# Retention's state update: one 64x64 matmul per head in two column groups instead of one 128x128 per pair of heads

## The chip, the cores and the metric

The kernel runs on one core of one Trainium2 chip. The metric is the device time of one execution in microseconds, and the times of several executions are summarised by their median. TensorE (PE) does the matmuls and holds a weight tile that is loaded separately (PEld); VectorE (DVE), ScalarE (ACT) and GpSimd (POOL) work on SBUF and PSUM; SyncE (SP) issues most of the DMA transfers.

## The reference, cut to what matters

The program is a trunk of two layers over 1024 tokens of width 1024. Each layer has a normalisation, one input projection, three groups of heads (windowed attention, retention, gated linear attention), an output projection and a residual. Retention has four heads with key and value width 64 and works in chunks of 128 tokens:

```python
def step(state, inp):
    qi, ki, vi = inp
    sc = jnp.einsum('bhid,bhjd->bhij', qi, ki) * dmask
    intra = jnp.einsum('bhij,bhjv->bhiv', sc, vi)
    inter = jnp.einsum('bhid,bhdv->bhiv', qi * q_decay, state)
    new_state = chunk_decay * state + jnp.einsum('bhjd,bhjv->bhdv', ki * k_decay, vi)
    return new_state, intra + inter
```

The part that the change touches is the last sum: for each head a product of k (128 tokens by 64) and v (128 tokens by 64), contracted over the tokens, added to a state of 64 by 64. There are eight chunks in each layer; after the last one no state is needed, so there are seven updates in each of two layers, 14 in all.

## The kernel before

All 1024 tokens are cut into eight tiles of 128, which are also retention's chunks. A layer runs in this order: the gates (`gg`, `rg`), then retention's projections `rq`, `rk`, `rv` for pairs of tiles, then those of the linear attention and the attention, their cores, and the output projection. The weights come from DRAM in pieces of 256 KB into staging tiles `st`, of which there are five, and are split there into a high part (L145 on ACT or L147 on DVE, a cast) and a low part (L489 on DVE or POOL, a subtraction), both kept in `arena`.

The order of TensorE's instructions is the order in which the program records them. Side work (a chunk of retention, of attention, a normalisation) is written as generators that are put into a list of jobs; a planning clock `clk` is advanced by a cost for every recorded matmul (in `mult` at L161) and transpose (L176), and a job goes on when the clock has reached its due time, taken from a table of latencies `L`. So the side work is laid between the projections' matmuls by hand-set costs. The order on the other engines is made by a scheduler from the recorded program.

A chunk of retention is the job `ret_core(l, t, q, k, v)`. Its steps are: four transposes of q and k into one PSUM tile (L176); a copy to SBUF by ACT (key `rT`, L145); after a planned delay the scores, four matmuls of 64 contracted rows (L161, shown as `aux<-t 64*128`); the causal mask by DVE (L1055); then, once the previous state is there, for each pair of heads q times the state `stR` and the scores times v; and then the state update.

`stR` holds two pairs of heads, each as a 128 by 128 tile: the head's 64 by 64 state stands on the diagonal, and the other two blocks stay zero, so that one matmul of 128 contracted rows serves both heads of a pair. The update before multiplies the k of a pair (128 columns) by the v of the pair (128 columns) into 128 by 128 of PSUM (`pst`), whose off-diagonal blocks are not used. DVE adds the upper left and the lower right blocks to `stR` (L1074, twice) and multiplies all of it by the chunk's decay (L1076). k carries the inverse decay already (L1033). After the chunk, `head_norm_gate` normalises the output, and ACT and DVE write a high and a low half (L145, L845), which SP stores to `mixS`.

Two other places use groups of columns already: the linear attention's state update (`gla_core`, four heads with 32 columns each) and attention's product of probabilities and v (two groups of 64 columns). Before the matmuls of retention's scores, ACT's copy `rT` has to be done; ACT runs its instructions in its own order, among them casts of weights, the copy of v (key `rv`) and the high halves for `mixS`, whose buffers must have been stored before they are written again.

Of the kernel before, what the change touches and what calls it, by code (L numbers as in the profile page):

```python
# [14 lines left out]
ALU = mybir.AluOpType  # L15
AX = mybir.AxisListType

P = 128
# [71 lines left out]
def trunk(ctx: ExitStack, tc: tile.TileContext, ins, cst, out):  # L90
    nc = tc.nc
    V, A, G, T = nc.vector, nc.scalar, nc.gpsimd, nc.tensor
# [16 lines left out]
    def t2(dt=F32):  # L109
        return gp.tile([P, 512], dt, tag="t2", name=nm("t2"), bufs=B2)  # L110

    def t1(dt=F32):
        return gp.tile([P, 256], dt, tag="t1", name=nm("t1"), bufs=B1)
# [10 lines left out]
    def aux(dt=F32):  # L124
        return ps.tile([P, 512], dt, tag="aux", name=nm("aux"), bufs=8 - MMB)
# [17 lines left out]
    def copy(k, dst, src):  # L143
        if EN[k] == "A":
            A.activation(dst, src, AF.Copy)  # L145
        else:
            V.tensor_copy(dst, src)  # L147

    def dma(k, dst, src):
        {"S": nc.sync, "A": A, "P": G}[EN[k]].dma_start(dst, src)  # L150

    def h4(ap):
        return ap.rearrange("p (h q) -> p h q", h=4)
# [6 lines left out]
    def mult(dst, lhsT, rhs, start, stop, cost=None):  # L160
        T.matmul(dst, lhsT, rhs, start=start, stop=stop)  # L161
        if cost is not None:
            clk[0] += cost
            return
        n = 1
        for d in rhs.shape[1:]:
            n *= d
        c = n / 2400.0
        if rhs.dtype == F32R:
            c = max(c, 0.107 if lhsT.shape[-1] > 64 else 0.055)  # L170
        else:
            c = max(4 * c, 0.21 if n > 2 else 0.03)
        clk[0] += c

    def transp(dst, src, idn):
        T.transpose(dst, src, idn)  # L176
        clk[0] += 0.056 if src.dtype == F32R else 0.109

    def lat(key, l):

        return L[key + "@1"] if l and key + "@1" in L else L[key]
# [4 lines left out]
    def flag(name, lat=0.0):  # L186
        flags[name] = clk[0] + lat
# [661 lines left out]
    def head_norm_gate(l, t, po, gate, scale, eps, kt0):  # L849

        sq = t1()
        A.activation(sq, po, AF.Square)
        ss = small(4)
        V.tensor_reduce(ss, h4(sq), AX.X, ALU.add)
        r = rstd_of(ss, 4, scale, eps)
        g1 = t1()
        V.tensor_tensor(h4(g1), h4(po), r.unsqueeze(2).to_broadcast((P, 4, 64)), ALU.mult)  # L857
        eng("hng").tensor_tensor(g1, g1, gate, ALU.mult)  # L858
        yield lat("hn1", l)
        pt = aux()  # L860
        for j in range(2):
            transp(pt[:, j * P:(j + 1) * P], g1[:, j * P:(j + 1) * P], ident)
        store_mix(t, kt0, pt[:, 0:256].rearrange("p (k q) -> p k q", k=2), 2)
        flag(("mix", l, t, kt0), lat("hn2", l))
# [171 lines left out]
    def ret_core(l, t, q, k, v):  # L1036
        yield lat("rc1", l)
        pt = aux()
        for j in range(2):
            transp(pt[:, j * P:(j + 1) * P], q[:, j * P:(j + 1) * P], ident)  # L1040
            transp(pt[:, (2 + j) * P:(3 + j) * P], k[:, j * P:(j + 1) * P], ident)
        tt_ = t2()
        qT = tt_[:, 0:256]
        kTt = tt_[:, 256:512]
        copy("rT", tt_, pt)
        yield lat("rc2", l)
        sp = [aux(), aux()]
        for h in range(4):
            r = slice(64 * (h % 2), 64 * (h % 2) + 64)
            c = slice((h // 2) * P, (h // 2) * P + P)  # L1050
            mult(sp[h % 2][:, c], kTt[r, c], qT[r, c], True, True)
        sc = t2()
        scv = h4(sc)
        for c in range(2):
            V.tensor_tensor(scv[:, c:4:2], sp[c][:, 0:256].rearrange("p (h q) -> p h q", h=2),  # L1055
                            causal.unsqueeze(1).to_broadcast((P, 2, P)), ALU.mult)
        yield lat("rc3", l)
        if t > 0:
            yield (0.0, ("stR", l, t))
        po = aux()  # L1060
        for j in range(2):
            if t > 0:
                mult(po[:, j * P:(j + 1) * P], qT[:, j * P:(j + 1) * P], stR[:, j, :], True, False)
            for h in (2 * j, 2 * j + 1):
                mult(po[:, 64 * h:64 * h + 64], sc[:, h * P:(h + 1) * P], v[:, 64 * h:64 * h + 64],
                     t == 0, t == 0 or h % 2 == 1)
        if t < NT - 1:
            pst = aux()
            for j in range(2):
                mult(pst[:, j * P:(j + 1) * P], k[:, j * P:(j + 1) * P], v[:, j * P:(j + 1) * P], True, True)  # L1070
            for c in range(2):
                r = slice(64 * c, 64 * c + 64)
                blk = stR[r, :, 64 * c:64 * c + 64]
                V.tensor_tensor(blk, blk, pst[r, 0:256].rearrange("p (j n) -> p j n", j=2)[:, :, 64 * c:64 * c + 64],  # L1074
                                ALU.add)
            V.tensor_tensor(stR, stR, cdt.unsqueeze(2).to_broadcast((P, 2, P)), ALU.mult)  # L1076
            flag(("stR", l, t + 1), lat("rc4", l))
        sg = t1()
        dma("lsr", sg, srS[t])
        yield from head_norm_gate(l, t, po[:, 0:256], sg, 4.0 / 64.0, 4.0 * EPS, 4)  # L1080
# [59 lines left out]
    def layer(l):  # L1140
# [35 lines left out]
        for p in range(NP_):  # L1176
            last = p == NP_ - 1
            rr = {}
            for name in ("rq", "rk", "rv"):
                w = unit(l, name)  # L1180
                for tt in range(2):
                    t = 2 * p + tt
                    pm = mm()
                    project(pm[:, 0:256], l, t, w)
                    src = pm[:, 0:256]
                    if name == "rv":
                        v = t1()
                        copy("rv", v, src)
                        job(ret_core(l, t, rr[("rq", tt)], rr[("rk", tt)], v))
                    else:  # L1190
                        rr[(name, tt)] = ret_rot(t, src, qdec if name == "rq" else kdec)
                    pump()
                if last:
                    load(l, {"rq": "gqk", "rk": "gv", "rv": "kv"}[name])
# [169 lines left out]
```

## Time and profile before

| | |
|---|---|
| median of 3 runs | 1022.42 us (1018.75 to 1022.86) |
| the profiled execution's own time | 1017.62 us |
| its span, first to last instruction | 1015.6 us |
| granted TensorE clock, mean | 0.988 |
| TensorE busy | 984.0 us, 97% of the span |
| VectorE, ScalarE, GpSimd busy | 641.1, 387.8, 279.7 us |
| HBM read and written | 102.42 and 34.60 MB |

A row of the timeline gives the start, the length, the engine, the line of the program, the operation, what it writes and reads, the shape (rows*columns of the weights, then partitions x moving columns), the count, and, in brackets, the idle time before it with what ended it. Neighbouring instructions of one kind are merged into one row. A row of groups gives the count, the busy time, the mean length in ns, and the idle time before. A line can be that of a helper: every matmul has L161, and every copy made through one helper has L145 or L147. Matmuls overlap, so a length says less than the distance between two starts. A matmul on fp32 operands leaves two records.

### The profile page before, as it was taken

What the parts mean: (1) busy time and instruction counts of PE and PEld (TensorE: products, weight loads), DVE (VectorE), ACT (ScalarE), POOL (GpSimd) and SP (SyncE); (2) the same over time, 40 slices, a digit from 0 to 9 for tenths busy, and PEclk for the clock granted to TensorE, in tenths of its full rate; (3) what the DMA queues carried; (4) which work ended last, traced back from release to release, by engine and by line L of the source; (5) the groups of instructions that cost most, each with busy time, mean ns of one, the idle gap of its engine ahead of it and who ended that gap; (6) DMA issues with size and microseconds to landing.
All of it is one profiled execution on the core that took longest, in us unless ns stands there. A gap on an engine that the chain in (4) does not pass through costs nothing.

```text
span 1015.6 us, 19469 instructions
## 1 busy us (share of the span) xinstructions
PE 984.0 (97%) x7185; PEld 837.6 (82%) x7185; DVE 641.1 (63%) x1567; ACT 387.8 (38%) x1112; POOL 279.7 (28%) x310
## 2 busy tenths in 40 slices
PE   5899999999999999999999999999999999999997
PEld 1599999888998777778889999988899877777886
DVE  3778856858656778754676285685666576563322
ACT  2477311233322655633454332133322266653111
POOL 2342011434320335522243020132333134532000
PEclk8999999999999999999999999999999999999999
DMA  9842513624226355687455161342122323436753
GB/s 320 283 132 78 162 58 99 175 74 120 79 72 187 89 141 177 189 270 228 166 159 164 47 177 32 94 139 81 53 91 74 114 89 95 139 118 202 230 188 143
DMA packets 124555, 140.39 MB, mean 138 GB/s; under 512 B 12990, under 2 KB 95784, under 8 KB 124460
## 3 DMA queue, kind: packets, MB, share of 16 engines
q1 hardware_dynamic: 118764, 129.53, 41.8%
q10 hardware_dynamic: 5696, 9.62, 2.6%
q8 instruction: 56, 0.92, 0.4%
q14 instruction: 39, 0.32, 0.1%
HBM read 102.42 MB, written 34.60 MB: 135 GB/s over the span
## 4 chain that ended last, share of the span: by engine, by line
PE 85%; DVE 5%; DMA 2%; ACT 1%; issue 1%; POOL 1%; DVEq 0%; POOLq 0%; SPq 0%; ACTq 0%
PE mm L161 65%; PE aux L161 15%; PE aux L176 5%; DMA st<-in_w_mod_dram 2%; DVE arena L489 1%; DVE acc L361 1%; POOL sm L525 0%; ACT t L145 0%; DVE arena L147 0%; DVE mx L997 0%; POOL arena L489 0%; DVE t L858 0%; DMA st<-in_w_in_dram 0%; ACT L899 0%; DVE t L963 0%
## 5 line engine op out<-in xcount | busy, mean ns | idle before, releaser
L161 PE MATMUL mm<-arena,arena 128*128 128x256 f32 (+2 forms) x1824 | 302.5, 319 | 2.8 <-DVE t L871 2.0
L161 PE MATMUL mm<-arena 128*128 128x256 f32 (+2 forms) x1824 | 298.6, 318 | 2.8 <-ACT arena L594 1.8
L161 PEld LDWEIGHTS mm<-arena,arena 128*128 128x128 f32 x1824 | 254.8, 190 | 28.4 <-issue 4.4
L161 PEld LDWEIGHTS mm<-arena 128*128 128x128 f32 x1824 | 255.2, 191 | 25.5 <-ACT arena L594 2.0
L161 PE MATMUL mm<-arena,mx 128*128 128x512 f32 (+1 forms) x816 | 184.4, 384 | 0.0
L161 PEld LDWEIGHTS mm<-arena,mx 128*128 128x128 f32 x816 | 145.6, 188 | 33.7 <-issue 1.9
L525 POOL TENSOR_TENSOR sm<-sm,mhalf 128x1 f32<-128x1 f32 (+1 forms) x64 | 53.0, 828 | 316.3 <-DVE sm L524 309.7
L489 POOL TENSOR_TENSOR arena<-st,arena 128x512 fp32r<-128x512 f32 x58 | 81.9, 1420 | 110.2 <-ACT arena L145 88.4
L145 ACT ACTIVATE t<-aux 128x256 f32<-128x256 f32 (+2 forms) x112 | 52.2, 471 | 94.3 <-PE aux L176 76.4
L813 POOL TENSOR_TENSOR smx<-smx,sm 128x512 f32<-128x512 f32 x32 | 36.2, 1131 | 139.1 <-DVE sm L812 114.7
L809 ACT ACTIVATE smx<-smx,sm 128x129 f32<-128x129 f32 x128 | 50.0, 393 | 44.8 <-DVE sm L806 42.1
L145 ACT ACTIVATE arena<-st 128x512 fp32r<-128x512 f32 x82 | 48.8, 625 | 44.7 <-PE mm L161 20.2
L361 DVE SCALAR_TENSOR_TENSOR acc<-st,c_act,acc 128x512 f32<-128x512 f32 x60 | 49.1, 818 | 22.8 <-DMA st<-in_w_mod_dram 22.5
L176 PE MATMUL aux<-c_ident,t 128*128 128x128 f32 x288 | 48.2, 286 | 8.4 <-DVE t L556 5.9
L1124 DVE SCALAR_TENSOR_TENSOR t<-t,sm,t 128x512 f32<-128x512 f32 x32 | 26.9, 876 | 41.2 <-DMA t<-xs 20.5
L489 DVE TENSOR_TENSOR arena<-st,arena 128x512 fp32r<-128x512 f32 x54 | 51.0, 958 | 2.7 <-ACT arena L145 1.3
L1089 DVE TENSOR_TENSOR t<-mm,modg 128x512 f32<-128x512 f32 x30 | 20.7, 688 | 47.7 <-ACT t L1088 47.2
L176 PEld LDWEIGHTS aux<-c_ident,t 128*128 128x128 f32 x288 | 35.3, 146 | 14.7 <-DVE t L556 7.3
L1088 ACT ACTIVATE t<-mm 128x512 f32<-128x512 f32 x30 | 17.9, 595 | 73.7 <-DVE t L1124 37.4
L161 PEld LDWEIGHTS aux<-t,mx 32*128 32x128 f32 (+1 forms) x896 | 40.2, 187 | 5.3 <-issue 2.8
L161 PE MATMUL aux<-t,mx 32*128 32x32 f32 (+1 forms) x896 | 41.5, 272 | 1.1 <-DVE t L857 0.9
L588 ACT ACTIVATE t<-aux,mod,mod 128x128 f32<-128x128 f32 x68 | 26.0, 457 | 41.8 <-PE aux L176 18.7
(193 smaller groups left out, 1253.3 us busy)
## 6 DMA issues: line engine op xcount, KB each, us to landing
st<-in_w_in_dram SPq DMA_DIRECT2D x96, 256.0 KB
st<-in_w_mod_dram SPq DMA_DIRECT2D x64, 256.0 KB
mx<-mixS SPq DMA_DIRECT2D x32, 512.0 KB
mixS<-t SPq DMA_DIRECT2D x64, 128.0 KB
st<-in_w_out_dram SPq DMA_DIRECT2D x32, 256.0 KB
mixS<-t SPq DMA_DIRECT2D x32, 256.0 KB
wm<-in_w_mod_dram SPq DMA_DIRECT2D x12, 512.0 KB
t<-in_x_dram SPq DMA_DIRECT2D x24, 256.0 KB
```

The lines of the kernel that those rows point to most:

```text
L145: A.activation(dst, src, AF.Copy)
L161: T.matmul(dst, lhsT, rhs, start=start, stop=stop)
L176: T.transpose(dst, src, idn)
L361: V.scalar_tensor_tensor(acc, wt, c_act[:, k:k + 1], acc, ALU.mult, ALU.add)
L489: (G if first == 0 else eng(f"wlo{kc}")).tensor_tensor(wt[:, 1, 2 * kc:2 * kc + 2, 0:256], st, f(hi), ALU.subtract)
L525: G.tensor_tensor(r, r, mhalf[:, :w], ALU.pow)
L588: A.activation(hf[:, ks], at[kt], AF.Identity, scale=gain, bias=shift)
L809: A.activation(sm[:, h, :], sm[:, h, :], AF.Exp, bias=mx[:, h:h + 1], accum_out=sums[:, h:h + 1])
L813: eng("pn").tensor_tensor(sm[:, :, 0:128], sm[:, :, 0:128], rs.unsqueeze(2).to_broadcast((P, 4, P)), ALU.mult)
L1088: A.activation(yg, pm, AF.Square, accum_out=ss[:, nh:nh + 1])
L1089: V.tensor_tensor(yg, pm, modg[l][:, 512 * nh:512 * nh + 512], ALU.mult)
L1124: V.scalar_tensor_tensor(xt[j], yg[j], r, xt[j], ALU.mult, ALU.add)
```

## The change

The change replaces the two matmuls of a chunk's update by four. Each multiplies the 64 k columns of one head by the 64 v columns of the same head. The head with even number writes PSUM partitions 0 to 63, the one with odd number 64 to 127, so that the two heads of a pair stand in two groups of columns of the array; the pair's index picks the PSUM columns. DVE reads the same number of elements as before, now from 128 columns of PSUM. The planning cost is given as 0.1067 for each of the four, 0.427 for a chunk; before, two matmuls had 0.2133 each by the rule in `mult`, 0.427 as well.

```diff
             pst = aux()
             for j in range(2):
-                mult(pst[:, j * P:(j + 1) * P], k[:, j * P:(j + 1) * P], v[:, j * P:(j + 1) * P], True, True)
+                for c in range(2):
+                    h = slice(P * j + 64 * c, P * j + 64 * c + 64)
+                    mult(pst[64 * c:64 * c + 64, 64 * j:64 * j + 64], k[:, h], v[:, h], True, True, 0.1067)
             for c in range(2):
                 r = slice(64 * c, 64 * c + 64)
                 blk = stR[r, :, 64 * c:64 * c + 64]
-                V.tensor_tensor(blk, blk, pst[r, 0:256].rearrange("p (j n) -> p j n", j=2)[:, :, 64 * c:64 * c + 64],
-                                ALU.add)
+                V.tensor_tensor(blk, blk, pst[r, 0:P].rearrange("p (j n) -> p j n", j=2), ALU.add)
             V.tensor_tensor(stR, stR, cdt.unsqueeze(2).to_broadcast((P, 2, P)), ALU.mult)
```

## The prediction

> **What bounds the kernel now.** I read the page first: its span, the busy shares and the chain that ended last.
>
> ```profile
> span 1015.6 us, 19469 instructions
> PE 984.0 (97%) x7185; PEld 837.6 (82%) x7185; DVE 641.1 (63%) x1567; ACT 387.8 (38%) x1112; POOL 279.7 (28%) x310
> PEclk8999999999999999999999999999999999999999
> PE 85%; DVE 5%; DMA 2%; ACT 1%; issue 1%; POOL 1%; DVEq 0%; POOLq 0%; SPq 0%; ACTq 0%
> ```
>
> TensorE is busy for 97% of the span, has its full clock after the start and holds 85% of the chain. A change of its instruction stream is therefore worth what it does to TensorE's own time, plus what it does to the few waits of TensorE. The changed lines run in two stretches only, so the next views are the busy times there and TensorE's waits there.
>
> ```profile
> 120.00:206.00 86.00, 84.58 (x690) 79.63 (x688) 57.51 (x168) 21.44 (x44) 17.27 (x16) 1.00 0.37 111
> 606.00:692.00 86.00, 83.77 (x683) 78.72 (x683) 58.48 (x167) 19.82 (x41) 16.03 (x14) 1.00 0.35 102
> ...
> PE aux L161 <- ACT t L145: 0.6, 1, 0.6
> PE aux L176 <- DVE t L1033: 0.6, 1, 0.6
> ...
> PE aux L161 <- ACT t L145: 1.5, 2, 0.9
> PE aux L176 <- DVE t L1033: 0.6, 1, 0.6
> ```
>
> The first two rows give per stretch its length and the busy time (instructions) of PE, weight loads, DVE, ACT and POOL. TensorE works 84.6 of 86 us and 83.8 of 86. The four others name what its waits come from (total, times, longest; first stretch, then second): ACT's copy of the transposed q and k (L145), and DVE's k decay (L1033). Nothing in either list waits for `stR`, so the state update itself has slack, and DVE's three instructions on `stR` stay what they are.
>
> **The instructions replaced.** A 128x128 fp32 matmul is two records in the trace, so 28 matmuls are the 56 of the next row. After the change there are 56 matmuls, 112 records, with 64 weight columns and 64 moving columns. The durations overlap; what counts is the distance between weight loads.
>
> ```profile
> L161 PE MATMUL aux<-t,t 128*128 128x128 f32 x56 | 9.3, 288 | 0.0
> ...
> 128.89 0.97 PEld L161 LDWEIGHTS aux<-t,t 128*128 128x128 f32 x8
> 129.78 0.30 PEld L161 LDWEIGHTS mm<-arena,arena 128*128 128x128 f32 x2
> ```
>
> These eight loads are four for score times v (64 moving columns), then four for the state update (128 moving columns), and the next matmul's load starts 0.89 us after the first: 0.111 us each, with 64 columns streamed as with 128. So the load sets the pace. The old update costs 4 x 0.111 = 0.445 us a chunk. A load of 64 columns I take at half, 0.055, and of 32 at 0.028.
>
> The new shape is not in this trace, but its two neighbours are: the state update of the gated linear attention (four groups of 32 columns, 64 moving) and attention's product with v (two groups of 64 columns, 256 moving).
>
> ```profile
> 229.13 0.98 PEld L161 LDWEIGHTS aux<-t,mx 128*128 128x128 f32 x8
> 230.18 0.16 PEld L161 LDWEIGHTS aux<-t,t 128*32 128x32 f32 x8
> 230.43 0.19 PEld L161 LDWEIGHTS mm<-arena 128*128 128x128 f32 x1
> ...
> 348.12 0.20 PEld L161 LDWEIGHTS aux<-t,va 128*64 128x64 f32 x4
> 348.70 0.19 PEld L161 LDWEIGHTS mm<-arena,arena 128*128 128x128 f32 x1 [0.39 <-issue]
> ...
> L161 PEld LDWEIGHTS aux<-t,vd 128*64 128x64 f32 x112 | 8.0, 137 | 4.0
> ```
>
> - Groups run at once: four loads of some 137 ns each lie within 0.20 us.
> - Going in costs: the last of the eight full loads is at 229.13 + 7 x 0.111 = 229.91, and the first narrow load comes 0.27 later, 0.16 more than the pace. The array seems to empty before the shape changes.
> - The stay, from first narrow load to next full load, is 0.25 with two records a group of 64 columns streamed, and 0.58 with two of 256. With s for 64 columns streamed and d for the way out: 0.028 + 2s + d = 0.25 and 0.055 + 8s + d = 0.58, so s = 0.05 and d = 0.12.
>
> The new update has four records a group (two pairs of heads, two records each): 0.055 + 4 x 0.05 + 0.12 = 0.38 if the loads hide, 0.39 if they pace it. With the way in: 0.16 + 0.385 = 0.545 against 0.445, **+0.10 us a chunk**. Bounds: -0.22 (half the old time, no way in or out) and +0.33 (the groups one after the other: 0.055 x 8 + 0.05 + 0.12 + 0.16 - 0.445, rounded). I take 0.10, since both neighbours show the groups at once and the switch.
>
> In three of the 14 chunks the next work already has another shape (64-row groups), so the way out was paid before:
>
> ```profile
> 197.77 0.97 PEld L161 LDWEIGHTS aux<-t,t 128*128 128x128 f32 x8
> 198.87 0.52 PEld L161 LDWEIGHTS aux<-t 64*128 64x128 f32 x8
> ...
> 634.35 0.97 PEld L161 LDWEIGHTS aux<-t,t 128*128 128x128 f32 x8
> 635.45 0.52 PEld L161 LDWEIGHTS aux<-t 64*128 64x128 f32 x8
> ...
> 685.88 0.72 PE L161 MATMUL aux<-t 64*128 64x128 f32 x8 [0.95 <-ACT t L145]
> ```
>
> From the eighth load (197.77 + 0.78 = 198.55) to the next it is 0.32, 0.21 over the pace; the new update is then 0.11 cheaper, at 198 and at 635. The third, before 685.88, is hidden by a wait of 0.95 for ACT: 0. TensorE's own part: 11 x 0.10 - 2 x 0.11 = **+0.9 us**.
>
> **What moves beside it.** TensorE's order is unchanged. The lists of the two programs differ on the other engines in a few places at the last two chunks of each layer.
>
> ```profile
> 188.01 2.71 SPq L150 DMA_DIRECT2D mixS<-t  x2
> 190.83 3.27 SPq L150 DMA_DIRECT2D st<-in_w_in_dram  x4
> ...
> 673.96 2.74 SPq L150 DMA_DIRECT2D mixS<-t  x2
> 676.82 0.37 SPq L150 DMA_DIRECT2D st<-in_w_mod_dram  x1
> ...
> 678.59 0.87 ACT L145 ACTIVATE t<-aux 128x256 fp32r<-128x256 f32 x2 [1.27 <-DMA mixS<-t]
> ...
> 679.51 0.72 PE L161 MATMUL aux<-t 64*128 64x128 f32 x8 [0.55 <-ACT t L145]
> ...
> 184.88 0.37 SPq L150 DMA_DIRECT2D st<-in_w_in_dram  x1
> 187.69 0.63 ACT L145 ACTIVATE arena<-st 128x512 fp32r<-128x512 f32 x1 [2.13 <-DMA st<-in_w_in_dram]
> ```
>
> SP puts a 256 KB weight load ahead of the second 128 KB `mixS` store, at 188 to 191 and 674 to 677. ACT waits for that store (1.27 us) before it writes the buffer again, the copy of the transposed q and k is behind it in ACT's line, and TensorE waits for that copy (0.55). This is the chain on which the store's delay would reach TensorE. Bounds: 0, if the load is too late to matter, and 2.8 us, a whole load from issue (184.88) to use (187.69). The store took about 2 us from issue to use (issue over at 676.70, ACT free at 678.59), so 128 KB more is worth some 0.8 us and a 256 KB load ahead at most about twice that; it is issued earlier than the store, so part of it has passed. I take 0.4 at each place: **+0.8 us**.
>
> ```profile
> 684.44 0.63 ACT L145 ACTIVATE arena<-st 128x512 fp32r<-128x512 f32 x1 [0.72 <-PE aux L161]
> 684.98 0.36 ACT L145 ACTIVATE t<-mm 128x256 f32<-128x256 f32 x1
> 685.24 0.59 ACT L145 ACTIVATE t<-aux 128x512 f32<-128x512 f32 x1
> ...
> 180.68 0.41 DVE L147 CAST arena<-st 128x512 fp32r<-128x512 f32 x1
> 186.09 1.45 DVE L489 TENSOR_TENSOR arena<-st,arena 128x512 fp32r<-128x512 f32 x1
> ```
>
> On ACT the copy of v (684.98) moves ahead of the cast at 684.44, which takes 0.26 us (685.24 - 684.98) out of the way of the copy on which TensorE waits 0.95. But on SP the load of that cast moves behind a store. From -0.3 to +0.8: I take 0. On DVE a cast of weights (0.41) moves some twelve instructions later, at 180.68 and its twin at 667, and the subtraction behind it goes into a busier place, where one took 1.45. That is -0.4 to +1.0 before the k decay; TensorE would then wait longer there and shorter for ACT just after: 0. Swaps of DVE's `stR` lines with the norm's small ones are hidden by the slack of `stR`; gone, they cost an instruction's 0.4 each.
>
> **Sum.** +0.9 + 0.8 = +1.7 us. The profiled execution took 1017.62 us (span 1015.6), 4.8 under the median of the runs, so the same program would profile at 1019.3, and on the median 1022.42 it is **1024.1 us**. What this kernel's measurement can tell from no change is 0.5%, 5.1 us.
>
> **Rivals.**
> - Packing for free. The column groups halve the update and the switches hide: 14 x -0.22 = -3.1, 1019.3. For it: the groups do overlap. Against it: the 0.27 before the narrow loads, in a stream with no wait. The Trainium skill, TensorEngine Tiling (Array Packing), section Theoretical Speedup, gives up to 2x for a small dimension of 64, which is this case; its section Key Properties says that a switch of mode drains the array. By the first sentence alone the sum is 1019.3, and the row at 230.18 sides with the second.
> - The store behind the load, at full price. At both places ACT, and so TensorE, waits a whole load longer: 0.9 + 2 x 2.8 = 6.5, 1028.9, slower. It decides from 2.1 us on at each place (0.9 + 4.2 = 5.1), which needs a load that leaves just before the store. For it: ACT's wait ends with that store already. Against it: the load may go as soon as its buffer is free, well ahead.
> - The groups don't overlap, so that the change doesn't do what it says: 14 x 0.33 = 4.6, 1027.0. Against it: the four loads within 0.20 us.
>
> **How the numbers follow.** Forecast 0.62, all within 0.5%. Free packing 0.12 (0.08 within, 0.04 faster, if the runs fall 2 us lower as well). Store at full price 0.14, slower. No overlap 0.06 (0.04 within, 0.02 slower). Another 0.06, a third to each side, is for a median of runs that lie 4 us apart (1018.75 to 1022.86). Together: faster 0.06, within 0.76, slower 0.18. The range 1018.8 to 1028.0 takes in free packing and no overlap, and leaves out most of the store at full price.
>
> **What would show it.** Right: loads 128*64 for `aux<-t,t`, eight a chunk, pairs together, 0.27 after the last full load and 0.38 to 0.39 before the next; TensorE's waits at 193 and 679 up by under a microsecond each. Wrong: the next full load under 0.25 after the first narrow one, or loads 0.055 apart; a wait of 2 us or more for ACT's copy; or a wait for `stR`, which I hold to have slack.

## The result, and the profile after

The changed kernel takes 1023.39 us (median of 20 runs, 1021.01 to 1027.17), the kernel before beside it 1020.21 us (20 runs, 1015.82 to 1023.70): a ratio of 1.0033, 95% interval 1.0020 to 1.0045. By the ratio that is some 3.4 us more, between 2.0 and 4.6 (the two medians differ by 3.18). It lies within the 0.5% of the forecast and above its +1.7 us.

The page of the changed kernel: span, busy times and the chain that ended last. Its profiled execution took 1025.8 us by its own time, 2.4 above its median, where that of the kernel before, 1017.62, lies 2.6 below the 1020.21 it had in these runs; so the 8.5 us between the two spans overstate the change, and the stretches below are the better guide.

```profile
span 1024.1 us, 19577 instructions
PE 986.1 (96%) x7241; PEld 838.0 (82%) x7241; DVE 641.6 (63%) x1567; ACT 388.5 (38%) x1112; POOL 282.1 (28%) x310
PE 80%; DVE 8%; DMA 2%; ACT 2%; issue 2%; POOL 1%; SPq 0%; DVEq 0%; POOLq 0%; ACTq 0%
```

TensorE's busy time grew by 2.1 us, but its share of the chain fell from 85% to 80% and DVE's rose from 5% to 8%: TensorE now waits for others. The waits of TensorE in the two stretches that were shown of before (first 120 to 206, then 606 to 705, which is longer than before's stretch because the last wait has moved out of it; total, times, longest):

```profile
PE aux L161 <- ACT t L145: 2.1, 1, 2.1
...
PE aux L161 <- ACT t L145: 4.6, 2, 2.4
```

The wait for ACT's copy rose from 0.6 to 2.1 us in layer 0 and from 1.5 to 4.6 in layer 1. Against that, the wait of 0.6 for the k decay (L1033), which stood in both stretches before, is gone. The tiles themselves, in the timeline of the weight loads and the groups of the page:

```profile
129.79 0.91 PEld L161 LDWEIGHTS aux<-t,t 128*128 128x128 f32 x12
130.76 0.89 PEld L161 LDWEIGHTS mm<-arena,arena 128*128 128x128 f32 x7
...
201.47 0.91 PEld L161 LDWEIGHTS aux<-t,t 128*128 128x128 f32 x12
202.45 0.52 PEld L161 LDWEIGHTS aux<-t 64*128 64x128 f32 x8
...
L161 PEld LDWEIGHTS aux<-t,t 128*64 128x64 f32 x112 | 4.4, 136 | 0.9
```

A row of twelve is the four full loads of score times v and the eight narrow ones. From its start to the next work it is 0.97 us, where it was 0.89 before; ahead of 64-row work it is 0.98, where it was 1.10 (197.77 to 198.87). To three digits it is nearly the same at every chunk: 0.082 or 0.083 us more at eleven, 0.118 or 0.119 less at two; at the third of these (691) a wait covers it. Together that is **+0.67 us** for the tiles. The way in is not a wait that the new program added: the update's first load waits on the same semaphore of TensorE's own in both kernels, and before it came at the usual 0.112 us.

The rest, as the experiments below will bear out, starts on DVE. This is the stretch of SP, DVE, ACT and TensorE in layer 0, and the rows of its twin in layer 1. First a row of before that was not shown, then the changed kernel's:

```profile
184.16 0.69 DVE L489 TENSOR_TENSOR arena<-st,arena 128x512 fp32r<-128x512 f32 x1
```

```profile
184.99 0.42 DVE L147 CAST arena<-st 128x512 fp32r<-128x512 f32 x1
186.31 0.43 DVE L857 TENSOR_TENSOR t<-aux,sm 128x256 f32<-128x256 f32 x1 [0.90 <-POOL sm L525]
186.57 1.30 POOL L489 TENSOR_TENSOR arena<-st,arena 128x512 fp32r<-128x512 f32 x1 [0.29 <-ACT t L145]
186.65 1.77 DVE L489 TENSOR_TENSOR arena<-st,arena 128x512 fp32r<-128x512 f32 x1
188.44 0.37 SPq L150 DMA_DIRECT2D st<-in_w_in_dram  x1
191.29 0.63 ACT L145 ACTIVATE arena<-st 128x512 fp32r<-128x512 f32 x1 [4.51 <-DMA st<-in_w_in_dram]
193.23 0.38 ACT L145 ACTIVATE t<-mm 128x256 f32<-128x256 f32 x1 [1.30 <-DMA mixS<-t]
194.79 0.87 ACT L145 ACTIVATE t<-aux 128x256 fp32r<-128x256 f32 x2 [1.18 <-DMA mixS<-t]
195.72 0.71 PE L161 MATMUL aux<-t 64*128 64x128 f32 x8 [2.09 <-ACT t L145]
...
676.73 1.70 DVE L489 TENSOR_TENSOR arena<-st,arena 128x512 fp32r<-128x512 f32 x1
...
685.84 0.72 PE L161 MATMUL aux<-t 64*128 64x128 f32 x8 [2.20 <-ACT t L145]
...
693.99 0.71 PE L161 MATMUL aux<-t 64*128 64x128 f32 x8 [2.41 <-ACT t L145]
```

The subtraction L489 is, by these times, the last reader of a staging buffer, and SP's next weight load into it leaves when it ends: 184.85 and 184.88 before, 188.42 and 188.44 after. The same weight loads of TensorE stand 1.23 us later at 180 us in this execution, so against TensorE's work the load is 2.3 us late. About 1.3 of these come from the place of the subtraction, behind the cast (moved) and behind the norm's L857, which waits 0.90 us for GpSimd; 1.1 come from its length, 1.77 for 0.69, since it now starts 0.08 us behind a subtraction of GpSimd. ACT's cast of these weights then holds ACT's line (4.51 us, before 2.13), two waits for stores follow it (1.30 and 1.18), and the copy on which TensorE waits is behind all of them. The subtraction's twin in layer 1 ends at 678.43, and two such waits come after it (2.20 and 2.41, where 0.55 and 0.95 stood before).

### The profile page after: what moved, and what is told of

Same layout as the page of the kernel before. It is cut to its first block, busy times and chain, and to the rows that moved or that the text cites. A ratio compares the mean times of both kernels' runs of the same rounds, so it can differ in the third digit from the quotient of the medians.

```text
span 1024.1 us, 19577 instructions
## 1 busy us (share of the span) xinstructions
PE 986.1 (96%) x7241; PEld 838.0 (82%) x7241; DVE 641.6 (63%) x1567; ACT 388.5 (38%) x1112; POOL 282.1 (28%) x310
## 4 chain that ended last, share of the span: by engine, by line
PE 80%; DVE 8%; DMA 2%; ACT 2%; issue 2%; POOL 1%; SPq 0%; DVEq 0%; POOLq 0%; ACTq 0%
PE mm L161 62%; PE aux L161 14%; PE aux L176 4%; DVE arena L489 1%; DMA st<-in_w_mod_dram 1%; POOL sm L525 1%; DVE t L590 1%; DMA st<-in_w_in_dram 0%; DVE acc L361 0%; DVE arena L598 0%; DVE t L871 0%; DVE t L1125 0%; DVE t L420 0%; DVE t L556 0%; ACT arena L145 0%
## 5 line engine op out<-in xcount | busy, mean ns | idle before, releaser
L489 POOL TENSOR_TENSOR arena<-st,arena 128x512 fp32r<-128x512 f32 x58 | 85.7, 1486 | 111.0 <-ACT arena L145 85.2
L489 DVE TENSOR_TENSOR arena<-st,arena 128x512 fp32r<-128x512 f32 x54 | 53.8, 1010 | 4.2 <-ACT arena L145 2.6
```

What stands on the lines that cost most here:

```text
L489: (G if first == 0 else eng(f"wlo{kc}")).tensor_tensor(wt[:, 1, 2 * kc:2 * kc + 2, 0:256], st, f(hi), ALU.subtract)
```

## The experiments

Theory A: the order on VectorE (the moved cast and the subtraction behind it) makes the weights late and costs most. Theory B: the shape of the matmuls costs it. Theory C: SP's and ACT's swapped rows cost it, as the forecast had it. Each kernel was timed beside the kernel before on the same chip, except where one execution is named. An order was pinned by edges without a semaphore between instructions of one engine, so that only the place in the engine's line changes. The helper is shown here; in the edits below the lists of pairs (`ORDER`) are put in words or as the rows that they move:

```diff
+def keep_order(tc):
+    made = {i.name: i for i in tc.nc.cur_bb.bb.instructions}
+    for pairs in ORDER.values():
+        for a, b in pairs:
+            tc.add_manual_dep(made[f"I-{b}"], f"I-{a}",
+                              mybir.DependencyInfo(mybir.DependencyClass.NoSync, mybir.DependencyReason.DATA),
+                              reason="order")
...
             trunk(tc, ins, cst, out)
+            keep_order(tc)
```

The table sums up the profiles. "Late" is the time of SP's load at 184.88 against TensorE's work, relative to before. The next two columns are the time that a stretch of TensorE's work takes more than in the kernel before, from the starts of the same weight loads (times of before). They hold waits, tiles and, in some executions, a fall of the granted clock (last section), so differences of a microsecond between two rows there prove nothing; the lateness of the load does not depend on it. A fall can also lie on either side of a stretch's end: the kernel before has one at 729 us, the changed kernel one at 696, and counted to 800 us the +4.39 is +3.4.

| kernel | matmuls | late, us | 180 to 215 | 665 to 715 | ratio to before |
|---|---|---|---|---|---|
| changed kernel | new | 2.33 | +2.66 | +4.39 | 1.0033 [1.0020, 1.0045] |
| e1 shape alone | new | -0.07 | +1.12 | +1.79 | 1.0016 [0.9989, 1.0043] |
| e2 order alone | old | 2.64 | +2.82 | +1.72 | 1.0044 [1.0021, 1.0066] |
| e3 order of VectorE | new | 2.34 | +2.50 | +2.84 | 1.0066 [1.0043, 1.0089] |
| e4 order of SP and ACT | new | -0.07 | +0.36 | +2.50 | 1.0003 [0.9972, 1.0033] |
| e5 before, copy first | old | 0.01 | -0.12 | 0.00 | 0.9993 [0.9968, 1.0019] |
| e6 after, copy first | new | 2.32 | +4.51 | +1.90 | 1.0031 [1.0009, 1.0054] |
| e7 cast back | new | 0.09 | +0.64 | +0.98 | 1.0021 [0.9994, 1.0047] |
| e8 groups in turn | new | -0.07 | -0.01 | +1.66 | one execution, 1021.78 us |
| e9 cast late alone | old | 2.35 | +1.94 | +4.39 | 1.0052 [1.0025, 1.0079] |
| e10 the same, layer 0 | old | 2.36 | +1.99 | +0.41 | 1.0001 [0.9979, 1.0023] |
| e11 subtraction first | new | 0.06 | +0.34 | -0.52 | 0.9990 [0.9968, 1.0012] |

**The shape without the order, and the order without the shape.** In e1 the changed matmuls run with the order of before on every other engine; in e2 the old matmuls run with the changed kernel's order. GpSimd's order is the same in both kernels.

```diff
 e1, on the changed kernel
+ORDER = order of the kernel before on VectorE, ScalarE, SyncE
 e2, on the kernel before
+ORDER = order of the changed kernel on VectorE, ScalarE, SyncE
```

> The four 64x64 matmuls stay, and DVE, ACT and SP run in the order that they had before, fixed by a list of pairs. Order theory: only the change of shape is left, 0.641 us from the last full load before the update to the first after it, against 0.558 before (+0.083) at 11 chunks, -0.12 at two, so +0.7 us, a ratio of 1.0005 to 1.001; the waits for ACT's copy (L145) go back to about 0.6 near 191 and 0.55 and 0.95 near 680. Shape theory (the new shape costs all of it, through something that the distances do not show): a ratio of 1.003, waits above 2 us as in the changed kernel.

> The two 128x128 matmuls of before, with DVE, ACT and SP in the order of the changed kernel. Order theory: the longer waits come with the order, 2.1 us for ACT's copy near 195, 2.2 and 2.4 near 685 and 693, in all some 5 us of waits there against 2.1 to 3.5 before, so +2 to +3 us and a ratio of 1.002 to 1.003. Shape theory: a ratio of 1.000, waits as before.

The order alone costs what the change costs (1.0044). The shape alone has 1.0016, and its interval holds both 1 and the change's 1.0033. So it is e2 that speaks against theory B here; e9 and e11 below do so more clearly. In e1 one row goes against the forecast, a wait of TensorE for the state (L1077 is the decay, a line further down than in the kernel before):

```profile
202.69 0.46 PE L161 MATMUL aux<-stR,t 128*128 128x128 f32 x2 [0.58 <-DVE stR L1077]
```

**Which engine's order.** e3 keeps the changed order on VectorE alone, e4 on SP and ScalarE alone; both have the new matmuls.

```diff
 e3, on the changed kernel
+ORDER = order of the kernel before on ScalarE, SyncE
 e4, on the changed kernel
+ORDER = order of the kernel before on VectorE
```

> The four 64x64 matmuls, ACT and SP in the order of before, DVE in the order of the changed kernel. If the loads ahead of the stores on SP are what makes ACT wait: as e1, a ratio of 1.001 at most. If the moved cast and subtraction on DVE are (they free a staging buffer later, so a weight load that goes out at 184.9 before goes out at 188.4, next to the stores): the waits stay at 2 us, a ratio of 1.002 to 1.003.

> The four 64x64 matmuls, DVE in the order of before, ACT and (but for two places) SP in the order of the changed kernel. If the loads ahead of the stores do it: the waits for ACT's copy stay above 1.5 us near 193 and 680, a ratio of 1.002 to 1.003. If DVE's moved cast does it: as e1, 1.001 at most.

```profile
193.92 0.71 PE L161 MATMUL aux<-t 64*128 64x128 f32 x8 [1.14 <-ACT t L145]
```

With VectorE's new order the load is late and the ratio 1.0066, above the change's own; why it is above is not shown. With SP's and ACT's order it is 1.0003, though that interval just reaches 1.0033. Theory C falls by e3: the loss is there with the old order on SP and ACT. The row of e4 above shows that the swaps are not free in the trace: TensorE waits 1.14 us in layer 0 (0.60 in e1) and 3.0 us once in layer 1 (2.2 in e1, in two waits). Their price in time is under what the runs can tell.

**The copy ahead of the store.** If TensorE waits only because the copy stands behind ACT's wait for a store, moving the copy forward takes the wait away. ScalarE's rows in e5 at one of the places (e6 has the same moves on the changed kernel):

```diff
 L145 Activation t<-mm 128x256
+L145 Activation t<-aux 128x512
 L145 Activation t<-aux 128x256
-L145 Activation t<-aux 128x512
 L145 Activation arena<-st 128x512
```

> The kernel before, with ACT's order alone changed in four places: the copy of q's transposes (rT, L145) is put ahead of the copy mh that waits for the staging buffer of the store, at the last chunk but one or so of each layer, and the v copy and rT ahead of two casts at the end of layer 1. Theory of the queue (ACT waits for a buffer that a store holds, and TensorE waits for a copy that only stands behind it): TensorE's waits for ACT's L145, 0.6 us between 185 and 215 and 1.5 us between 600 and 705 in the kernel before, go to under 0.5 together; time 1.5 us shorter at most, ratio to before 0.998 to 1.000. Rival (the copy is late for its own input, the store only ends last by the records): the waits stay at 0.6 and 1.5, ratio 1.000 to 1.001.

> The same moves on ACT in the changed kernel, everything else in its order. Theory of the order (the extra time over the tiles' own +0.7 us is TensorE waiting for the copy behind the wait for the store): the waits for L145 fall from 2.1 us (185 to 215) and 4.6 us (600 to 705) to under 1 us in all, and the ratio to before is 0.998 to 1.001. Rival of the tiles (the extra is in the matmuls' shape): waits fall and the time stays, ratio 1.002 to 1.0045. Rival of the late load (what is late is the weights of the load that now goes out at 188, not the store): TensorE waits as long for weights (DVE L147 or L489, or a DMA) instead, ratio about 1.003.

In the kernel before, the wait goes as expected. Among TensorE's waits of e5 (first stretch, then second) those for ACT's copy fell from 2.1 us in all to 0.2; but new are short ones for the mask (L1055) and the state (L1076, its decay), and the table's two stretches are hardly shorter (-0.12 and 0.00):

```profile
PE aux L161 <- ACT t L145: 0.2, 1, 0.2
...
PE aux L161 <- DVE t L1055: 0.7, 2, 0.4
...
PE aux L161 <- DVE stR L1076: 0.3, 1, 0.3
```

In the changed kernel it does not help (1.0031). ACT and TensorE in e6:

```profile
190.89 0.63 ACT L145 ACTIVATE arena<-st 128x512 fp32r<-128x512 f32 x1 [4.50 <-DMA st<-in_w_in_dram]
193.22 0.59 ACT L145 ACTIVATE t<-aux 128x512 f32<-128x512 f32 x1
...
197.78 1.30 ACT L145 ACTIVATE arena<-st 128x512 fp32r<-128x512 f32 x2 [3.04 <-DMA st<-in_w_in_dram]
...
201.34 1.22 PE L161 MATMUL aux<-t 64*128 64x128 f32 x8 [2.22 <-ACT t L145]
```

The copy at 193.22 no longer waits for a store. TensorE's wait at this chunk falls to 0.64, and the next chunk's copy, behind two casts that wait 3.04 us for weights, makes it wait 2.22. So the store, which the trace names as ending ACT's wait at 193.23 and 194.79, was only the nearest of the late things; behind it the weights are late too. Of the three ways written down for e6 the third comes nearest, though TensorE waits for ACT's copy and, in layer 1, 1.79 us for the mask, and not for the weights themselves.

**The cast put back, and the cast late alone.** e7 is the changed kernel with the cast, and the subtractions around it, where they stood before; e9 is the kernel before with just these rows moved as the change moves them, and e10 does so in layer 0 alone. The rows of VectorE in e9 (the moves of e7 are the reverse):

```diff
-L147 TensorCopy arena<-st 128x512
+L707 TensorTensor t<-mm,sincos 128x256
 L1033 TensorTensor t<-t,c_qdec 128x256
-L707 TensorTensor t<-mm,sincos 128x256
...
 L524 TensorScalarPtr sm<-sm 128x4
+L147 TensorCopy arena<-st 128x512
+L857 TensorTensor t<-aux,sm 128x256
 L489 TensorTensor arena<-st,arena 128x512
-L857 TensorTensor t<-aux,sm 128x256
+L858 TensorTensor t<-t,t 128x256
 L489 TensorTensor arena<-st,arena 128x512
-L858 TensorTensor t<-t,t 128x256
```

> The changed kernel with one thing put back on VectorE in each layer: the cast L147 that the change moved 12 places later (and the subtractions L489 around it) stands where it stood before; the other moved rows of VectorE, ScalarE and SyncE stay as the change has them. If that one cast is the cause: SP's weight load goes out at 184.6 to 185 again in place of 188.4, TensorE's wait for L145 in layer 0 is 0.6 to 1.1 in place of 2.1, layer 1 1.5 to 3, and the ratio to before is 0.999 to 1.0025 (as with the whole order of before on VectorE: 1.0003 and 1.0016). If the other swaps of VectorE (rows of stR and of the norm) are the cause: load at 184.6 or not, the waits stay at 2.1 and 4.6 and the ratio at 1.003 to 1.0065.

> The kernel before with one thing of the changed one, and none of its matmuls: on VectorE the cast L147 of a staged weight block stands 12 places later in each layer (and the subtractions L489 and the two norm rows L857 and L858 around it as the change has them); every other row of every engine as before. Theory of the cast: SP's load of 256 KB goes out at 188.0 to 188.5 in place of 184.88, the weights behind it come some 3 us later, TensorE waits for L145 about 2 us between 185 and 215 and 2 to 4.6 us between 600 and 705, and the ratio to before is 1.002 to 1.0045. Rival (the late cast costs only together with the other moved rows, on SP or ScalarE): the load is late and the waits for L145 stay at 0.6 and 1.5, ratio 0.999 to 1.001. Rival (the matmuls' shape carries it): as before, 1.000.

> The same in layer 0 only; layer 1 in the order of before. Theory of the cast: TensorE waits for L145 some 2 us between 185 and 215, and 1.5 us between 600 and 705 as before; the ratio is about half of the way of both layers, 1.001 to 1.0025. If one layer carries nearly all: ratio as before (0.999 to 1.001) or as with both (1.003 and more).

In e9 the subtraction, the load and ACT's cast are late as in the changed kernel, though no matmul was touched. The long wait comes one chunk later than there, as in e6; the first chunk's is 0.90:

```profile
185.61 1.55 DVE L489 TENSOR_TENSOR arena<-st,arena 128x512 fp32r<-128x512 f32 x1
187.18 0.37 SPq L150 DMA_DIRECT2D st<-in_w_in_dram  x1
190.07 0.63 ACT L145 ACTIVATE arena<-st 128x512 fp32r<-128x512 f32 x1 [4.54 <-DMA st<-in_w_in_dram]
193.26 0.71 PE L161 MATMUL aux<-t 64*128 64x128 f32 x8 [0.90 <-ACT t L145]
...
200.59 0.71 PE L161 MATMUL aux<-t 64*128 64x128 f32 x8 [1.97 <-ACT t L145]
```

Its ratio, 1.0052, is that of the change or above. In e7 the same chain is back in place, and the load leaves level with before (183.72, in an execution whose work stands 1.25 us earlier):

```profile
183.00 0.69 DVE L489 TENSOR_TENSOR arena<-st,arena 128x512 fp32r<-128x512 f32 x1
183.72 0.37 SPq L150 DMA_DIRECT2D st<-in_w_in_dram  x1
186.42 0.63 ACT L145 ACTIVATE arena<-st 128x512 fp32r<-128x512 f32 x1 [2.11 <-DMA st<-in_w_in_dram]
```

The two stretches of e7 cost 0.64 and 0.98 us in place of 2.66 and 4.39, of which some 1.5 us each are falls of the clock; e9 has +1.94 in the first without a fall. The ratio of e7, 1.0021 [0.9994, 1.0047], fits the theory but does not exclude the change's own 1.0033. e10 shows the same wait in layer 0 (+1.99) and next to none in layer 1 (+0.41); its ratio, 1.0001 [0.9979, 1.0023], came out at the low end, so that the runs do not split the cost between the layers.

**The subtraction's place.** The last run tells the twelve places of the cast from the place of the subtraction behind it: everything as in the changed kernel, the cast late, but the subtraction ahead of the norm's row, in both layers.

```diff
 L147 TensorCopy arena<-st 128x512
+L489 TensorTensor arena<-st,arena 128x512
 L857 TensorTensor t<-aux,sm 128x256
-L489 TensorTensor arena<-st,arena 128x512
+L489 TensorTensor arena<-st,arena 128x512
 L858 TensorTensor t<-t,t 128x256
-L489 TensorTensor arena<-st,arena 128x512
```

> The changed kernel with the cast L147 left late, and in each layer only two neighbours on VectorE exchanged back, twice: the subtraction L489 ahead of the norm's L857, and the next one ahead of L858. In the changed kernel the subtraction stands behind L857, which waits 0.90 us for GpSimd, and then starts 0.08 us after a subtraction of GpSimd and takes 1.77 us in place of 0.69; SP's load leaves 0.02 us after it ends (188.42, 188.44). Theory of the subtraction's place: it runs at 185.4, in the time in which VectorE waits for GpSimd, takes 0.69, and the load goes out at 186.1 in the changed kernel's time, level with the kernel before against TensorE's stream (184.88 + 1.23 = 186.1), 2.3 us sooner; the waits for L145 fall to those of the cast put back (about 1 us in the first stretch, 2 in the second), ratio to before 0.999 to 1.0025. Rival (the twelve places of the cast are what costs): the load stays 1 us or more late, waits 2 us and 4 us, ratio 1.003 or more.

```profile
184.25 0.42 DVE L147 CAST arena<-st 128x512 fp32r<-128x512 f32 x1
184.71 0.69 DVE L489 TENSOR_TENSOR arena<-st,arena 128x512 fp32r<-128x512 f32 x1
185.43 0.37 SPq L150 DMA_DIRECT2D st<-in_w_in_dram  x1
185.57 0.43 DVE L857 TENSOR_TENSOR t<-aux,sm 128x256 f32<-128x256 f32 x1 [0.17 <-POOL sm L525]
194.55 0.71 PE L161 MATMUL aux<-t 64*128 64x128 f32 x8 [1.70 <-ACT t L145]
```

The subtraction fits into the time in which VectorE waited for GpSimd, takes 0.69 again, and the load leaves level with before. The ratio is 0.9990 [0.9968, 1.0012]: no loss is left that the runs can tell, with the new matmuls, the late cast and the swapped rows of SP and ACT still there. The kernel before took longer in these runs than in others (1022.05 us; 1019.65 beside e9 on the same chip); against all its 39 runs there (1020.34) e11 is 0.4 us longer, which leaves room for the tiles' 0.67. One wait for ACT's copy is left in each stretch (1.70 and 1.80 us, against the 1 and 2 that were expected), and the one of 2.41 at the end of layer 1 is gone. The rival (the cast's twelve places) falls. This kernel and e5 are level with the kernel before, not shown to be faster than it.

**Groups one after the other.** One execution of the changed kernel with its loops exchanged and the order of before elsewhere.

```diff
-            for j in range(2):
-                for c in range(2):
+            for c in range(2):
+                for j in range(2):
```

> The changed kernel with the loops over c and j exchanged, so that the two matmuls of one column group stand next to each other and the groups come one after the other; order of the other engines as in the kernel before. If the groups overlap only when their matmuls alternate: the narrow loads come about 55 ns apart, not in pairs of 6 and 49, and from the last full load before to the next after them it takes about 0.2 us a chunk more than the 0.641 us of the changed kernel (0.84 to 0.86), 2.2 us in all. If what runs side by side does not depend on the order: 0.64 as now.

```profile
129.21 0.92 PEld L161 LDWEIGHTS aux<-t,t 128*128 128x128 f32 x12
130.19 1.24 PEld L161 LDWEIGHTS mm<-arena,arena 128*128 128x128 f32 x10
```

0.98 us in place of 0.97: the narrow loads still come in pairs, 14 ns apart where they were 6 or 7, and the distance to the next full load is 0.648 us for 0.641. So the overlap does not depend on whether the program alternates the groups, and the first expectation was wrong. The records do not name the column group, so that the pairs are of different groups is inferred.

## Why the prediction was right, and where it was not

- The time came close, 1023.39 us for 1024.1, by luck: the kernel before ran 2.2 us lower in these runs than in the three of the forecast, and that nearly made up for the change costing more than was forecast, 3.4 us (2.0 to 4.6) for 1.7. Of the two halves of the sum the tiles were right in their mechanism; the other was too small and missed the main cause.
- TensorE's own part was close in every piece: way in 0.27 and measured 0.26, stay 0.38 to 0.39 and measured 0.381, groups at once. The sum, +0.9, came out at +0.67, because these small differences make 0.10 a chunk of what is 0.083. The way in could have been read right: in the row at 229.13 the eighth load starts at 229.924 and not at 229.91, so the distance to the narrow load was 0.26 there too.
- Packing for free falls: the way in is there at all 14 chunks. The groups one after the other fall too.
- "SP puts a 256 KB weight load ahead of the second `mixS` store", +0.4 at each place: the place and the chain to TensorE were right (store, ACT's buffer, ACT's copy, TensorE), and the traces show a price of about that size. With these swaps and the load on time the first wait of layer 0 is 1.14 us in e4 and 1.10 in e7, against 0.61 before and 0.60 in e1 (the 0.8 us for 128 KB, from which the 0.4 was taken, stands in no row). In layer 1 the swaps make the first wait longer and the second shorter (1.65 and 0.25 us in e7, 0.79 and 1.41 in e1), and in the time they can't be told (e4).
- What this term missed is what the late load adds: the waits grew by 1.5 at 195.72, by 1.65 at 685.84 and by 1.46 at 693.99; the last was not in the sum at all, as the copy of v ahead of a cast was to even it out. The second store does not leave late: it goes at 191.11, 0.5 us sooner against TensorE's work than before (190.40). But ACT has the buffer only at 194.79, 3.7 us on, where it was 2.8 in e4 and at most 2.3 before. A wait of 2 us or more for ACT's copy was named as what would show the forecast wrong, and it came.
- The step that failed is the one on DVE: "a cast of weights moves some twelve instructions later, and the subtraction behind it goes into a busier place, where one took 1.45", priced at -0.4 to +1.0 and taken as 0. Its price was looked for on DVE, ahead of the k decay, and there the move even saved TensorE's wait of 0.6. What hangs on it is the staging buffer: the load that refills it leaves 0.02 to 0.03 us after the subtraction, so its 2.3 us reach SP, ACT and TensorE. e9 shows that moving these rows is enough for the loss, e11 that with the subtraction put ahead of the norm's row no loss can be told.
- "Nothing waits for `stR`" holds in the changed kernel. But TensorE waits for it 0.6 us in e1, where the waits for ACT are about those of the kernel before, and 0.3 in e5, where they are gone: the slack was smaller than "nothing waits" made it look.
- What stays open: the runs do not say why the scheduler, given the same planning cost for the update, put the cast later, nor do they divide the cost between the layers, or between the stores that land late and the weights that come late.

## What to carry to other kernels

When a change reorders an off-path engine, look for the last reader of each rotating buffer among the moved rows and follow it to the load that it releases: the price is the lateness of that load, not the row's own length. A wait that names one releaser may have several late things behind it; moving the waiting row forward (e6) tells whether it was the only one. A small change of shape is best run once with the old order pinned, so that the scheduler's answer to it is priced apart.

## What the runs showed of the hardware

- A subtraction L489 on VectorE takes 0.68 us when it is alone or starts first, and up to 1.79 when an instruction of GpSimd is running at its start (in the kernel before, all 31 that did not start into GpSimd's work took 0.67 to 0.69, the 23 others 0.68 to 1.79). In the changed kernel a start 0.08 us too late cost 1.08 us. The Trainium skill, GPSIMD Engine Reference, section Specifications, says that GpSimd shares its SBUF interfaces with VectorE, with contention for VectorE instructions that have two SBUF inputs; the subtraction is one, and the rows agree. No instruction of GpSimd in these traces reads or writes a PSUM tile (`aux`, `mm`); what was said of SBUF and PSUM ahead of the kernel holds here for VectorE and ScalarE.
- TensorE's granted clock falls to half for 3.4 us at a time in the middle of the program, in the kernel before too (at 545 and 729). In windows of the changed kernel (length, busy times of PE, weight loads, DVE, ACT and POOL, then the clock):

```profile
190.00:197.30 7.30, 4.99 (x41) 4.59 (x42) 7.20 (x19) 1.89 (x4) 3.28 (x1) 1.00 0.57 162
197.30:200.70 3.40, 3.40 (x12) 2.73 (x11) 1.72 (x3) 1.59 (x3) 1.28 (x1) 0.51 1.04 340
```

The fall follows the wait of 2.09 us that begins at 193.6. Over it TensorE's loads go from 2.1 to 3.7 us behind those of before, so it costs some 1.6 us, as much as the wait's growth of 1.5; it is part of the +2.66 in the table. It does not come every time: e9 and e10 wait 2 us near 200 without it, and show one at 264 and 267 instead, at a wait of 0.94 that passes without one in the kernel before. So what sets it off is not shown. The Trainium skill, TensorE: Matmul & The Clock Gate, part 1, puts the fall after about one idle window of 3.4 us that runs freely; the length of the pieces agrees, but here falls came at waits of 0.9 to 3.0 us.

The number of such falls goes with much of the scatter between executions: over the 31 runs of the kernel before beside e1, 0.001 less of the mean granted clock goes with 1.0 us more. It does not make the change's 3.4 us: the mean granted clock is 0.987 over the 20 runs of the changed kernel, and 0.987 over the 99 runs of the kernel before beside the experiments.
